# Loading x in three groups of blocks, with a norm for each group, in a two-layer decoder trunk

## The chip, the cores and the metric

The kernel runs on one core of one Trainium2 chip. The core has five engines with instruction streams of their own: TensorE (PE; its weight loads are shown as PEld), VectorE (DVE), ScalarE (ACT), GpSimd (POOL) and SyncE (SP, which here only issues DMAs). Each engine takes its instructions in the order in which they stand in its stream and waits on semaphores for the others. The metric is the time of one execution on the device, in microseconds; lower is better.

## The reference

One inference step of a trunk of two layers, for a prompt of 1024 positions and a decode batch of 8, with 1024 features. Layer 0 mixes with a gated linear recurrence (HGRN2), layer 1 with sliding-window attention; each layer has a SwiGLU feed-forward part. Every sub-layer is modulated by a conditioning vector `c`. What matters here is the very start: norm, modulation and first projection of layer 0.

```
def modulate(x, g, shift, scale):
    y = rms_norm(x, g) * (1.0 + scale[:, None, :]) + shift[:, None, :]
def ada_params(c, w, b):
    return (jax.nn.silu(c) @ w + b).astype(jnp.float32)
...
sh1, sc1, g1, sh2, sc2, g2 = jnp.split(ada_params(c, w_ada[l], b_ada[l]), 6, axis=-1)
xn = modulate(h, norm_w[l, 0], sh1, sc1)
...
q, f_raw, i, g = jnp.split(xn @ w_in, 4, axis=-1)      # the first projection, 1024 -> 4096
```

## The kernel before

**Tiling.** The 1024 prompt positions and the 8 decode positions stand side by side as 1032 columns; features lie on the 128 partitions, in `KT` = 8 row tiles `k`. For the first projection the columns are cut into three chunks `c` of 344 (`G3`). x is loaded in eight blocks of 128 positions, `xt[0]` to `xt[7]` (`load_x`, L380), and turned on PE into the feature-major tiles `h[k]` (`turn_x`, L451: per `k` one transpose for each block, then one DVE copy, L457, out of the bank).

**First norm.** ACT squares each block and sums it (`first_square`, L861). DVE makes one over the root by `newton` (L540, eleven small instructions behind the one of L887), puts the results on a diagonal (`dg`, L891), PE multiplies that by ones (L907) so that every partition has the factor of each column, and ACT copies it to `N.R` (L908). Before, this is done once for all eight blocks.

**Conditioning.** Shift and scale of layer 0 come from `w_ada`, loaded as 16 tiles of 512 KB in two halves: `wa[0]` gives them for the row tiles 0 to 3, `wa[1]` for 4 to 7. `first_step(i, k)` (L498) multiplies one tile, two matmuls; `first_end(i)` (L512) copies the result (L514), transposes it (L517) and leaves shift and scale in `ada` and `modA` (L522 to L530).

**Rows.** `N.apply_steps` (L732) makes the modulated input of one chunk, row tile by row tile: DVE L738, ACT L742 (high part), DVE L743 (low part). High and low parts are tiles of `X` (16 of them). Each `next` on it does two row tiles; a chunk's first four therefore need `wa[0]` alone.

**Projection.** Weights are streamed in units of 512 KB (`Stream`, `split_unit`, L191). A unit is loaded into one of three `raw` buffers and converted in two halves by `weight` (L179): ACT casts the high part (L182), POOL subtracts to get the low part (L185). For the first four units the conversion is held back (`held`) and called by hand. Units 0 to 3 are the four parts (f, v, q, g) of head 0. Each product is three matmuls (`mm3`, L282 to L285): high by high, high by low, low by high. In `hgrn_first` (L963) `part(c, i)` is unit `i` for chunk `c` over the first four row tiles, twelve matmuls; its accumulator stays in a PSUM bank, of tag `mm` or, for (1, 0) and (1, 1), of tag `ax`. Six parts are done this way, then, with the second conditioning half, the rest.

**What sets the order.** A planner puts the instructions of each engine in an order: it goes by the order of the text, but lets a later instruction go first where it holds the earlier one to be not ready yet. Three things bind it. `tc.keep_in_program_order(i)` pins an instruction behind the one that stands before it in the text on the same engine; the casts L182 of the first four units are pinned so. Buffers of one tag are handed out in the order of the text of the tiles' first instructions: a tile of a later line gets its buffer only after all the tiles of that tag from earlier lines have theirs. The tags here are `c4` (34 buffers of about 4 KB a partition: x blocks, `wa`, `h`, `X`), `raw` (3), `mm` (4 PSUM banks) and `ax` (4 PSUM banks). And DMAs of SP go through eight semaphores in turn, so that an issue waits for the landing of the one eight before it.

Before, x blocks 0 to 2 are loaded, then 3 to 7, then unit 0, the eight tiles of `wa[0]`, units 1 and 2, and four tiles of `wa[1]`; the other four follow at L899, where `turn_x(6, 2)` has been done and a `c4` buffer is free.

Of the kernel before, what the change touches and what calls it, by code (L numbers as in the profile page):

```python
# [57 lines left out]
def bc(ap, axis, n):  # L58
    u = ap.unsqueeze(axis)
    shape = list(u.shape)  # L60
    shape[axis] = n
    return u.to_broadcast(shape)
# [3 lines left out]
def trunk_kernel(  # L66
# [313 lines left out]
    def load_x(tb):  # L380
        t = big(cols=D)
        sp.dma_start(t, x_prompt[0, tb * P : (tb + 1) * P, :])
        xt.append(t)
# [8 lines left out]
    act.dma_start(pr2[40:48, :], final_norm_w.rearrange("(k f) -> k f", f=P))  # L392
    act.dma_start(pr2[48:56, :], lb_a.rearrange("l (k f) -> (l k) f", f=P))
    act.dma_start(pr2[56:57, :], gnorm_a)
    for tb in range(3, 8):
        load_x(tb)


    def first_half(k, i, t):
        src = w_ada[0][k * P : (k + 1) * P, 0:2048].rearrange("p (s n) -> p s n", s=2)  # L400
        sp.dma_start(t.rearrange("p (s n) -> p s n", s=2), src[:, :, i * 512 : (i + 1) * 512])
        return t
# [3 lines left out]
    for kk in range(4):  # L406
        t = big(cols=1024)
        wa[0].append(first_half(2 * kk, 0, t))
        t = big(cols=1024)
        wa[0].append(first_half(2 * kk + 1, 0, t))  # L410
    ws.ahead(3)
    for k in range(4):
        t = big(cols=1024)
# [37 lines left out]
    def turn_x(t0, n):  # L451
        for k in range(KT):
            ps = mmp() if k % 2 else axp()
            for j in range(n):
                pe.transpose(ps[:, j * P : (j + 1) * P], xt[t0 + j][:, k * P : (k + 1) * P], ident)
            dst = h[k][:, t0 * P : (t0 + n) * P]
            dve.tensor_copy(dst, ps[:, : n * P])  # L457

# [399 lines left out]
    dve.memset(ms, 1.0)  # L858

    def first_square(tb):  # L860
        act.activation(junk[:, :T], xt[tb], AF.Square, accum_out=ms[:, tb : tb + 1])  # L861

    act.activation(junk[:NB, :T], xd_in, AF.Square, accum_out=ms[:NB, 8:9])
    for tb in range(3):
        first_square(tb)
    turn_x(0, 3)
    for tb in range(3, 6):
        first_square(tb)
    turn_x(3, 3)
    for tb in range(6, 8):  # L870
        first_square(tb)
    held.pop(0)()


# [9 lines left out]
    dve.tensor_tensor(lb, lbe, lbe, op=ALU.subtract)  # L884
    dve.tensor_scalar(omlb, lb, -1.0, 1.0, op0=ALU.mult, op1=ALU.add)

    dve.tensor_scalar(ms, ms, 1.0 / D, EPS, op0=ALU.mult, op1=ALU.add)  # L887
    newton(y, ms, 9, P, "n")
    for half in range(2):
        s = slice(512 * half, 512 * half + 512)  # L890
        dve.tensor_tensor(  # L891
            dg[:, s].rearrange("p (j q) -> p j q", j=4),
            bc(ident, 1, 4),
            bc(y[:, 4 * half : 4 * half + 4], 2, P),
            op=ALU.mult,
        )
    dve.tensor_tensor(dg[:NB, T:TOK], ident[:NB, :NB], y[:NB, 8:9].to_broadcast([NB, NB]), op=ALU.mult)
    turn_x(6, 2)
    for k in range(4, KT):  # L899
        wa[1].append(first_half(k, 1, big(cols=1024)))  # L900
    ws.ahead(4)
    for k in range(2):
        first_step(0, k)
    for half in range(2):
        s = slice(512 * half, 512 * half + 512)
        ps = axp()
        pe.matmul(ps, ones, dg[:, s], start=True, stop=True)  # L907
        act.copy(N.R[:, s], ps)  # L908
    ps = axp()
    pe.matmul(ps[:, :NB], ones[:NB, :], dg[:NB, T:TOK], start=True, stop=True)  # L910
    act.copy(N.R[:, T:TOK], ps[:, :NB])
    for k in range(2, KT):
        first_step(0, k)
    first_end(0)
    X = Rows(KT)
    steps = [N.apply_steps(c, 0, X) for c in range(NCH)]
    held.pop(0)()
    for c in range(2):
        for _ in range(2):
            next(steps[c])  # L920
        if c == 0:
            held.pop(0)()


    osc = dp.tile([NH, P, T], F32, name="osc")
    odec = cst.tile([P, NH, NB], F32, name="odec")
# [34 lines left out]
            yield from ada_end(hh)  # L961

    def hgrn_first():  # L963
        us = ws.done[:4]
        acc = {}

        def part(c, i):
            acc[c, i] = axp() if c and i < 2 else mmp()
            proj(acc[c, i][:, :W], us[i], X, c, 0, 4)

        for c, i in ((0, 0), (0, 1), (0, 2), (1, 0)):
            part(c, i)
        for k in range(KT):
            first_step(1, k)
        part(1, 1)
        first_end(1)
        part(1, 2)
        held.pop(0)()
        for st in steps:
            for _ in st:  # L980
                pass
        for _ in us:
            ws.next()
        f, kk, v, q, g = (big() for _ in range(5))
        for c in range(NCH):
            s = G3.all(c)
            for i, t in enumerate((f, v, q, g)):
                ps = acc.get((c, i))
                if ps is None:
                    ps = mmp()  # L990
                    proj(ps[:, :W], us[i], X, c)
                else:
                    proj(ps[:, :W], us[i], X, c, 4, KT)
                if t is v:
                    act.copy(t[:, s], ps[:, :W])
                else:
                    act.activation(t[:, s], ps[:, :W], AF.Sigmoid)
                if t is q or t is g:
                    dve.tensor_tensor(t[:, s], t[:, s], ps[:, :W], op=ALU.mult)
        forget(0, f, kk)  # L1000
        data[0] = [f, kk, v, q, g]
        yield
# [1049 lines left out]
```

## Time and profile before

| | |
|---|---|
| time, three runs | 2525.5, 2527.67 and 2528.7 us; median 2527.67 |
| profiled execution | 2529.57 us, of which the span from the first to the last instruction is 2527.8 |
| mean granted TensorE clock | 0.992 |
| moved by DMA | 293.41 MB, mean 116 GB/s |
| read from HBM, written to it | 231.27 MB, 63.99 MB |

The profile shows one execution. Times are in microseconds from the first instruction. In the timeline a row has its start, its length, the engine, the line, the operation, what it writes and reads, shapes, and in brackets how long the engine had been idle and what ended that. `SPq` is SyncE issuing DMAs. Buffer numbers are left out: `c` stands for tiles of tag `c4`, `wu` for converted weights. Rows of the same line that follow each other without a gap are merged, with their count (`x8`). PE counts an fp32 matmul as several instructions.

### The profile page before, as it was taken

Reading aid. Unit: us, or ns where it says so; the run is one execution under the profiler, and the core shown is the slowest. Engines: PE = TensorE matmul, PEld = TensorE weight load, DVE = VectorE, ACT = ScalarE, POOL = GpSimd, SP = SyncE. Lnnn points to the kernel's source line nnn. Section 1 sums busy time; section 2 is a strip of 40 time slices with the busy share of each in tenths; the row PEclk is TensorE's granted clock in tenths of the full one; section 3 lists DMA queues with packets and bytes.
Section 4 is the critical chain, followed back from the end, with each engine's and each line's share of the span. In section 5 each row is a group of like instructions: output and inputs, shape, how many; then the busy total and the mean of one; then the engine's idle time right before and its main releaser. Section 6 shows DMA issues by size and latency. Waiting matters only on the chain.

```text
span 2527.8 us, 52251 instructions
## 1 busy us (share of the span) xinstructions
PE 2469.5 (98%) x21579; PEld 2346.0 (93%) x21579; DVE 1366.9 (54%) x3117; ACT 878.7 (35%) x1929; POOL 797.3 (32%) x577
## 2 busy tenths in 40 slices
PE   7999999999999999999999999999899999999998
PEld 4989999987889999999999997878899999999998
DVE  5444555564574555656433725566845555555436
ACT  4323333331363332333211655454633333333112
POOL 2211222220334444444432231102334444445321
PEclk9999999999999999999999999999999999999999
DMA  8564222248942223226321322523222222264201
GB/s 317 188 213 138 72 78 69 69 149 286 284 126 78 81 85 116 89 89 229 123 76 54 89 55 59 155 88 109 76 70 82 84 76 76 76 230 145 69 26 68
DMA packets 314495, 293.41 MB, mean 116 GB/s; under 512 B 28617, under 2 KB 291674, under 8 KB 314226
## 3 DMA queue, kind: packets, MB, share of 16 engines
q1 hardware_dynamic: 313856, 289.86, 35.5%
q8 instruction: 170, 2.79, 0.4%
q14 instruction: 67, 0.55, 0.1%
q10 hardware_dynamic: 402, 0.22, 0.0%
HBM read 231.27 MB, written 63.99 MB: 117 GB/s over the span
## 4 chain that ended last, share of the span: by engine, by line
PE 89%; DVE 5%; DMA 2%; issue 2%; SPq 1%; ACT 0%; POOL 0%; DVEq 0%; POOLq 0%; ACTq 0%
PE mm L283 20%; PE mm L285 20%; PE mm L284 20%; PE ax L283 6%; PE ax L284 6%; PE ax L285 6%; PE ax L473 2%; PE ax L1798 1%; PE ax L1869 1%; PE ax L1043 1%; PE ax L1855 1%; DVE c L1064 1%; PE ax L1132 1%; PE ax L1169 1%; DVE hs L809 1%
## 5 line engine op out<-in xcount | busy, mean ns | idle before, releaser
L185 POOL TENSOR_TENSOR wu<-raw,wu 128x512 fp32r<-128x512 f32 x460 | 626.2, 1368 | 1354.8 <-ACT wu L182 1118.7
L283 PE MATMUL mm<-c,wu 128*128 128x344 f32 (+1 forms) x2096 | 669.9, 320 | 6.0 <-ACT c L742 4.1
L285 PE MATMUL mm<-c,wu 128*128 128x344 f32 (+1 forms) x2096 | 658.7, 314 | 1.7 <-POOL wu L185 1.7
L284 PE MATMUL mm<-c,wu 128*128 128x344 f32 (+1 forms) x2096 | 658.7, 314 | 0.1
L182 ACT CAST wu<-raw 128x512 fp32r<-128x512 f32 x460 | 283.3, 620 | 705.9 <-PE mm L285 377.0
L283 PEld LDWEIGHTS mm<-c,wu 128*128 128x128 f32 x2096 | 395.6, 189 | 20.0 <-issue 10.3
L283 PE MATMUL mm<-xq,wu 128*128 128x258 f32 x1448 | 412.2, 285 | 1.0 <-ACT wu L182 1.0
L285 PE MATMUL mm<-xq,wu 128*128 128x258 f32 x1448 | 409.9, 283 | 0.8 <-POOL wu L185 0.8
L284 PE MATMUL mm<-xq,wu 128*128 128x258 f32 x1448 | 410.3, 283 | 0.0
L285 PEld LDWEIGHTS mm<-c,wu 128*128 128x128 f32 x2096 | 395.6, 189 | 6.2 <-issue 4.1
L284 PEld LDWEIGHTS mm<-c,wu 128*128 128x128 f32 x2096 | 396.2, 189 | 4.3 <-issue 3.4
L283 PE MATMUL ax<-xq,wu 128*128 128x258 f32 x1064 | 301.4, 283 | 0.0
L284 PE MATMUL ax<-xq,wu 128*128 128x258 f32 x1064 | 300.9, 283 | 0.0
L285 PE MATMUL ax<-xq,wu 128*128 128x258 f32 x1064 | 300.6, 283 | 0.0
L285 PEld LDWEIGHTS mm<-xq,wu 128*128 128x128 f32 x1448 | 275.2, 190 | 2.3 <-issue 1.2
L283 PEld LDWEIGHTS mm<-xq,wu 128*128 128x128 f32 x1448 | 274.5, 190 | 2.0 <-ACT wu L182 1.2
L284 PEld LDWEIGHTS mm<-xq,wu 128*128 128x128 f32 x1448 | 275.4, 190 | 0.1
L844 DVE SCALAR_TENSOR_TENSOR hs<-mm,ada,hs 128x344 f32<-128x344 f32 (+3 forms) x228 | 120.5, 532 | 183.8 <-PE mm L285 170.8
L284 PEld LDWEIGHTS ax<-xq,wu 128*128 128x128 f32 x1064 | 202.3, 190 | 0.0
L285 PEld LDWEIGHTS ax<-xq,wu 128*128 128x128 f32 x1064 | 201.6, 190 | 0.0
L283 PEld LDWEIGHTS ax<-xq,wu 128*128 128x128 f32 x1064 | 201.0, 189 | 0.0
L844 DVE SCALAR_TENSOR_TENSOR c<-mm,ada,c 128x344 f32<-128x344 f32 (+1 forms) x132 | 74.9, 571 | 111.3 <-PE mm L285 110.6
(323 smaller groups left out, 3596.1 us busy)
## 6 DMA issues: line engine op xcount, KB each, us to landing
c<-in_w_ada_dram SPq DMA_DIRECT2D x96, 512.0 KB
raw<-in_w_ffn_in_dram SPq DMA_DIRECT2D x152, 256.0 KB
ff<-c SPq DMA_DIRECT2D x44, 516.0 KB
c<-ff SPq DMA_DIRECT2D x44, 516.0 KB
raw<-in_w_ffn_out_dram SPq DMA_DIRECT2D x44, 512.0 KB
raw<-in_w_in_a_dram SPq DMA_DIRECT2D x32, 512.0 KB
hs<-hs SPq DMA_DIRECT2D x16, 516.0 KB
out_dram<-c SPq DMA_DIRECT2D x16, 512.0 KB
```

What stands on the lines that cost most here:

```text
L182: i = act.copy(u[:, 0, :], src)
L185: eng.tensor_tensor(u[:, 1, :], src, u[:, 0, :], op=ALU.subtract)
L283: pe.matmul(ps, wh, xh, start=first, stop=False)
L284: pe.matmul(ps, wh, xl, start=False, stop=False)
L285: pe.matmul(ps, wl, xh, start=False, stop=last)
L473: pe.matmul(ada_ps[q][32 * j : 32 * j + 32, 256 * i : 256 * i + 256], cT[:, k, :], u[i][:, j, :], start=(k == 0 and i == 0), stop=(k == KT ...
L809: dve.tensor_tensor(t, t, bc(R, 1, t.shape[1]), op=ALU.mult)
L844: dve.scalar_tensor_tensor(hc, ps[:, : g.pl[c]], ada[:, gate + n, 0:1], hc, op0=ALU.mult, op1=ALU.add)
L1043: pe.matmul(ps[32 * j : 32 * j + 32, c * 32 : (c + 1) * 32], KS[:, t0 : t0 + 32], QP[:, t0 : t0 + 32], start=True, stop=True, tile_positio ...
L1064: dve.tensor_tensor(q4[:, :, 1, :], q4[:, :, 1, :], bc(p3[:, :, 0], 2, M), op=ALU.mult)
L1132: pe.matmul(ps[:, j * P : (j + 1) * P], kt[:, s], vt[:, s], start=True, stop=True)
L1169: pe.matmul(o, attT[:, c, :], vt[:, s], start=(c == 0), stop=True)
```

## The change

x is loaded in three groups: blocks 0 to 2, 3 to 5, 6 and 7. Behind the first group come unit 0 and the eight `wa[0]` tiles; the second group stands behind those, then unit 1, the third group, unit 2 and the first four tiles of `wa[1]`. Each group gets its squares, its transposes and a norm of its own (`first_rows`, which replaces L863 to L871 and L887 to L911 with the same instructions on fewer columns): group one at the old place, group two behind the first four rows of chunk 0, group three inside `hgrn_first`, behind `part(0, 1)`. In groups two and three the squares and transposes are pinned with `keep_in_program_order`. Unit 1 is converted behind the second group's norm, unit 2 behind the third's, and the last four tiles of `wa[1]` and unit 3 are loaded behind that. All eight `first_step(0, k)` stand together. The decode positions' factor is made with the third group. What is computed is the same.

```diff
@@ -392,8 +392,6 @@
     act.dma_start(pr2[40:48, :], final_norm_w.rearrange("(k f) -> k f", f=P))
     act.dma_start(pr2[48:56, :], lb_a.rearrange("l (k f) -> (l k) f", f=P))
     act.dma_start(pr2[56:57, :], gnorm_a)
-    for tb in range(3, 8):
-        load_x(tb)
 
 
     def first_half(k, i, t):
@@ -408,6 +406,11 @@
         wa[0].append(first_half(2 * kk, 0, t))
         t = big(cols=1024)
         wa[0].append(first_half(2 * kk + 1, 0, t))
+    for tb in range(3, 6):
+        load_x(tb)
+    ws.ahead(2)
+    for tb in range(6, 8):
+        load_x(tb)
     ws.ahead(3)
     for k in range(4):
         t = big(cols=1024)
@@ -452,7 +455,9 @@
         for k in range(KT):
             ps = mmp() if k % 2 else axp()
             for j in range(n):
-                pe.transpose(ps[:, j * P : (j + 1) * P], xt[t0 + j][:, k * P : (k + 1) * P], ident)
+                i = pe.transpose(ps[:, j * P : (j + 1) * P], xt[t0 + j][:, k * P : (k + 1) * P], ident)
+                if t0:
+                    tc.keep_in_program_order(i)
             dst = h[k][:, t0 * P : (t0 + n) * P]
             dve.tensor_copy(dst, ps[:, : n * P])
 
@@ -858,17 +863,39 @@
     dve.memset(ms, 1.0)
 
     def first_square(tb):
-        act.activation(junk[:, :T], xt[tb], AF.Square, accum_out=ms[:, tb : tb + 1])
+        return act.activation(junk[:, :T], xt[tb], AF.Square, accum_out=ms[:, tb : tb + 1])
 
     act.activation(junk[:NB, :T], xd_in, AF.Square, accum_out=ms[:NB, 8:9])
-    for tb in range(3):
-        first_square(tb)
-    turn_x(0, 3)
-    for tb in range(3, 6):
-        first_square(tb)
-    turn_x(3, 3)
-    for tb in range(6, 8):
-        first_square(tb)
+
+    def first_rows(t0, n):
+
+
+        for tb in range(t0, t0 + n):
+            i = first_square(tb)
+            if t0:
+                tc.keep_in_program_order(i)
+        turn_x(t0, n)
+        dec = t0 + n == 8
+        w = n + dec
+        v, yv = ms[:, t0 : t0 + w], y[:, t0 : t0 + w]
+        dve.tensor_scalar(v, v, 1.0 / D, EPS, op0=ALU.mult, op1=ALU.add)
+        newton(yv, v, w, P, "n")
+        s = slice(t0 * P, (t0 + n) * P)
+        dve.tensor_tensor(
+            dg[:, s].rearrange("p (j q) -> p j q", j=n), bc(ident, 1, n), bc(yv[:, :n], 2, P), op=ALU.mult
+        )
+        ps = axp()
+        pe.matmul(ps[:, : n * P], ones, dg[:, s], start=True, stop=True)
+        act.copy(N.R[:, s], ps[:, : n * P])
+        if dec:
+            dve.tensor_tensor(
+                dg[:NB, T:TOK], ident[:NB, :NB], y[:NB, 8:9].to_broadcast([NB, NB]), op=ALU.mult
+            )
+            ps = axp()
+            pe.matmul(ps[:, :NB], ones[:NB, :], dg[:NB, T:TOK], start=True, stop=True)
+            act.copy(N.R[:, T:TOK], ps[:, :NB])
+
+    first_rows(0, 3)
     held.pop(0)()
 
 
@@ -884,43 +911,17 @@
     dve.tensor_tensor(lb, lbe, lbe, op=ALU.subtract)
     dve.tensor_scalar(omlb, lb, -1.0, 1.0, op0=ALU.mult, op1=ALU.add)
 
-    dve.tensor_scalar(ms, ms, 1.0 / D, EPS, op0=ALU.mult, op1=ALU.add)
-    newton(y, ms, 9, P, "n")
-    for half in range(2):
-        s = slice(512 * half, 512 * half + 512)
-        dve.tensor_tensor(
-            dg[:, s].rearrange("p (j q) -> p j q", j=4),
-            bc(ident, 1, 4),
-            bc(y[:, 4 * half : 4 * half + 4], 2, P),
-            op=ALU.mult,
-        )
-    dve.tensor_tensor(dg[:NB, T:TOK], ident[:NB, :NB], y[:NB, 8:9].to_broadcast([NB, NB]), op=ALU.mult)
-    turn_x(6, 2)
-    for k in range(4, KT):
-        wa[1].append(first_half(k, 1, big(cols=1024)))
-    ws.ahead(4)
-    for k in range(2):
-        first_step(0, k)
-    for half in range(2):
-        s = slice(512 * half, 512 * half + 512)
-        ps = axp()
-        pe.matmul(ps, ones, dg[:, s], start=True, stop=True)
-        act.copy(N.R[:, s], ps)
-    ps = axp()
-    pe.matmul(ps[:, :NB], ones[:NB, :], dg[:NB, T:TOK], start=True, stop=True)
-    act.copy(N.R[:, T:TOK], ps[:, :NB])
-    for k in range(2, KT):
+    for k in range(KT):
         first_step(0, k)
     first_end(0)
     X = Rows(KT)
     steps = [N.apply_steps(c, 0, X) for c in range(NCH)]
+    for _ in range(2):
+        next(steps[0])
+    first_rows(3, 3)
     held.pop(0)()
-    for c in range(2):
-        for _ in range(2):
-            next(steps[c])
-        if c == 0:
-            held.pop(0)()
-
+    for _ in range(2):
+        next(steps[1])
 
     osc = dp.tile([NH, P, T], F32, name="osc")
     odec = cst.tile([P, NH, NB], F32, name="odec")
@@ -961,15 +962,21 @@
             yield from ada_end(hh)
 
     def hgrn_first():
-        us = ws.done[:4]
         acc = {}
 
         def part(c, i):
             acc[c, i] = axp() if c and i < 2 else mmp()
-            proj(acc[c, i][:, :W], us[i], X, c, 0, 4)
-
-        for c, i in ((0, 0), (0, 1), (0, 2), (1, 0)):
-            part(c, i)
+            proj(acc[c, i][:, :W], ws.done[i], X, c, 0, 4)
+
+        part(0, 0)
+        part(0, 1)
+        first_rows(6, 2)
+        held.pop(0)()
+        for k in range(4, KT):
+            wa[1].append(first_half(k, 1, big(cols=1024)))
+        ws.ahead(4)
+        part(0, 2)
+        part(1, 0)
         for k in range(KT):
             first_step(1, k)
         part(1, 1)
@@ -979,8 +986,7 @@
         for st in steps:
             for _ in st:
                 pass
-        for _ in us:
-            ws.next()
+        us = [ws.next() for _ in range(4)]
         f, kk, v, q, g = (big() for _ in range(5))
         for c in range(NCH):
             s = G3.all(c)
```

## The prediction

> **What bounds the kernel now.** I read the page first, then busy time by stretch, then the timeline.
>
> ```profile
> span 2527.8 us, 52251 instructions
> ...
> PE 2469.5 (98%) x21579; PEld 2346.0 (93%) x21579; DVE 1366.9 (54%) x3117; ACT 878.7 (35%) x1929; POOL 797.3 (32%) x577
> ...
> PE 89%; DVE 5%; DMA 2%; issue 2%; SPq 1%; ACT 0%; POOL 0%; DVEq 0%; POOLq 0%; ACTq 0%
> ```
>
> TensorE carries the span. An edit of the start can only shorten or lengthen the time in which PE has nothing to do. The stretches (length, then busy time of PE, PEld, DVE, ACT, POOL, the granted clock, DMA share, GB/s):
>
> ```profile
> 9.20:24.50 15.30, 14.49 (x86) 10.22 (x85) 13.61 (x36) 12.65 (x22) 2.50 (x2) 1.00 1.03 389
> 24.50:38.40 13.90, 7.09 (x26) 1.96 (x26) 5.63 (x18) 3.40 (x8) 3.37 (x3) 1.00 0.90 306
> 38.40:46.22 7.82, 6.07 (x26) 5.41 (x26) 6.65 (x14) 4.57 (x9) 5.33 (x2) 0.78 0.64 221
> 46.22:59.12 12.90, 12.20 (x82) 8.70 (x83) 2.44 (x6) 2.26 (x5) 3.74 (x3) 1.00 1.00 340
> 59.12:100.00 40.88, 40.77 (x260) 40.45 (x261) 21.09 (x50) 21.55 (x48) 9.88 (x8) 1.00 0.40 141
> ```
>
> From 59.12 on PE has no gap, so what counts is how early that state is reached, with how much work done. The way there, in the timeline:
>
> ```profile
> 9.65 9.01 SPq L401 DMA_DIRECT2D c<-in_w_ada_dram  x8
> 30.14 1.05 PE L503 MATMUL ax<-c,cT 128*32 128x512 f32 x4 [0.26 <-DMA c<-in_w_ada_dram]
> 33.68 0.60 ACT L514 COPY c<-ax 128x512 f32<-128x512 f32 x1
> 36.23 2.48 DVE L738 SCALAR_TENSOR_TENSOR w<-c,modA,c 128x344 f32<-128x344 f32 x3
> 38.40 0.90 PE L283 MATMUL mm<-c,wu 128*128 128x344 f32 x2 [3.41 <-ACT c L742]
> 46.22 0.42 PE L285 MATMUL mm<-c,wu 128*128 128x344 f32 x1 [1.75 <-POOL wu L185]
> 47.91 0.32 PE L283 MATMUL ax<-c,wu 128*128 128x344 f32 x1
> 49.64 0.32 PE L285 MATMUL ax<-c,wu 128*128 128x344 f32 x1
> 49.89 4.12 PE L503 MATMUL ax<-c,cT 128*32 128x512 f32 x32
> 59.12 0.74 PE L283 MATMUL mm<-c,wu 128*128 128x344 f32 x3 [0.70 <-ACT c L742]
> 59.97 0.42 PE L284 MATMUL mm<-c,wu 128*128 128x344 f32 x1
> ```
>
> The first conditioning half waits for its eight tiles until 30.14; projections start at 38.40; the second half's matmuls run at 49.89; its X rows reach PE at 59.12. One `part` is twelve matmuls, 47.91 to 49.64 for eleven steps, so 1.9 us. Between 59.12 and 59.97 three matmuls run where that pace allows 5.4: the gapless state counts from 59.5.
>
> **The change, part by part.** *Loads.* Five x blocks (512 KB each) go behind the eight tiles. At 389 GB/s they are 6.7 us, so the last tile lands at 23.4 and its matmuls (1.05) end at 24.5. L514 to the first L738 is 2.55 (33.68 to 36.23). L514 no longer stands behind the norm's copies (2.5, from 31.19), since group one's norm is done while tiles load. First L738 at 27.0, against 36.23: this is the change's gain, 9.2 us at this point.
>
> *What is queued behind it now.* Before, all eight squares, copies and the norm ran under the load wait. Now five blocks' work follows. Prices:
>
> ```profile
> 10.16 1.06 ACT L861 ACTIVATE c<-c 128x1024 f32<-128x1024 f32 x1
> 18.44 1.06 ACT L861 ACTIVATE c<-c 128x1024 f32<-128x1024 f32 x1
> 14.82 0.56 DVE L457 COPY c<-mm 128x384 f32<-128x384 f32 x1
> 18.54 0.54 DVE L457 COPY c<-mm 128x384 f32<-128x384 f32 x1
> 19.01 0.41 DVE L457 COPY c<-ax 128x256 f32<-128x256 f32 x1
> 20.33 0.41 DVE L457 COPY c<-ax 128x256 f32<-128x256 f32 x1
> 23.36 0.15 DVE L550 SCALAR_TENSOR_TENSOR nt<-ny 128x9 f32<-128x9 f32 x1
> 24.97 0.17 DVE L552 SCALAR_TENSOR_TENSOR ny<-nt,ny 128x9 f32<-128x9 f32 x1
> 25.25 0.69 DVE L891 TENSOR_TENSOR c<-ident,ny 128x512 f32<-128x512 f32 x1
> 31.12 1.98 PE L907 MATMUL ax<-c,ones 128*128 128x512 f32 x4
> 32.28 0.59 ACT L908 COPY c<-ax 128x512 f32<-128x512 f32 x1 [10.14 <-PE ax L907]
> 41.07 0.56 DVE L738 SCALAR_TENSOR_TENSOR w<-c,modA,c 128x344 f32<-128x344 f32 x1
> 43.02 2.03 DVE L743 SCALAR_TENSOR_TENSOR c<-w,ada,c 128x344 fp32r<-128x344 f32 x4
> 40.88 6.53 POOL L185 TENSOR_TENSOR wu<-raw,wu 128x512 fp32r<-128x512 f32 x2 [2.63 <-ACT wu L182]
> 20.18 2.50 POOL L185 TENSOR_TENSOR wu<-raw,wu 128x512 fp32r<-128x512 f32 x2 [18.41 <-ACT wu L182]
> ```
>
> Start to start: a square 1.18 (seven steps, 10.16 to 18.44); a three-block copy 0.465 (eight, 14.82 to 18.54), eight of them 3.7; a two-block copy 0.33 (four), eight 2.6; a norm's chain 0.20 a step (eight, 23.36 to 24.97), twelve steps 2.4; the diagonal 0.69 per 512 columns; its matmul half of 1.98 per 512; its copy 0.59. Four rows of X are eight DVE instructions, 41.07 to 45.05: 4.0.
>
> Estimates from these, in order, on DVE unless said: rows of chunk 0 to 31.0; copies of blocks 3 to 5 to 34.7 (their squares are pinned behind the fourth L742, three times 1.18, and are covered); norm and diagonal 2.9 to 37.6; matmul 0.75 and copy 0.45 to 38.8; rows of chunk 1 to 42.8.
>
> The weights are pinned too:
>
> ```profile
> 19.49 1.12 ACT L182 CAST wu<-raw 128x512 fp32r<-128x512 f32 x2
> 34.16 1.16 ACT L182 CAST wu<-raw 128x512 fp32r<-128x512 f32 x2
> 25.49 6.03 SPq L401 DMA_DIRECT2D c<-in_w_ada_dram  x4
> 34.88 2.48 POOL L185 TENSOR_TENSOR wu<-raw,wu 128x512 fp32r<-128x512 f32 x2 [12.20 <-ACT wu L182]
> 37.30 0.95 POOL L928 MEMSET c<- 128x1024 f32 x1
> 39.99 2.53 SPq L401 DMA_DIRECT2D c<-in_w_ada_dram  x4
> ```
>
> Unit 0's cast waited for the last square, unit 1's for L514. Now unit 1's cast stands behind the second norm's copy (38.8) and unit 2's behind the third. Unit 1's POOL half then meets chunk 1's rows on DVE. Before, that meeting took 6.53 for two passes against 2.50 alone, and `part` (0,2) got its half only at 46.22, 1.2 after DVE stopped (45.05). So (0,1) gets its half at 44.0 and ends at 45.6 (ten matmuls, 1.6). Blocks 6 and 7 are pinned behind (0,1) on PE and behind chunk 1's fourth L742 on ACT: a first transposed pair 0.2 later, copies end at 48.4, norm and diagonals (2.9) at 51.3, matmuls (0.7) at 52.0. R for the last chunk is not needed at once.
>
> The second conditioning half cannot slip ahead. Buffers of a tag go out in the order of the text: L928 has no input, yet POOL, idle 12.20 before unit 1's pass, runs it only after that, at 37.30, behind X's sixteen tiles; the first four second-half tiles were issued from 25.49, yet L503 came at 49.89, behind (1,0), which takes the `ax` bank before it. In the changed text (1,0) and that bank stand behind the third norm's two `ax` banks. So from 52.0 PE still has (0,2), (1,0), the half's 4.1, (1,1), four transposes (0.4) and (1,2): 12.1 us, gapless, to 64.1. The next rows come beside it: 52.0+1.9+4.1+2.55 is 60.6 for L738, 2.2 more (36.23 to 38.40) to PE, 62.8. At 59.5 before, all of that was done.
>
> *Clock.* PE would idle about 4.0 us before 52.0. The only idle time here that halved the clock is the 5.0 before 38.40 (0.78 over 7.82, so 1.7 lost); the 0.70 before 59.12 did not. The price lies between 0 and 1.7; 4.0 is nearer to 5.0, so 1.7. The Trainium skill ("TensorE: Matmul & The Clock Gate", section on HAM oscillation) warns of idle gaps above some 3.4 us; by that rule this change adds three such gaps, and without it the sum would be 1.7 lower.
>
> *At no cost.* On SP, units 1 and 2 now stand between x groups. At 512 KB in 1.35 us (389 GB/s), blocks 3 to 5 land at 27.4, unit 1 at 28.8, blocks 6 and 7 at 31.5, unit 2 at 32.8; they are wanted at 31.0, 38.8, 45.6 and 52, so the waits above cover them; without that cover each would delay its step by its lateness. The last four second-half tiles are issued later in the text, behind L928's buffer. The SP rows show four issues at 39.99 to 42.5, their matmuls done by 54.0; here they are needed at about 56. Cover gone, each microsecond late costs one. The two extra norms' instructions (24 at 0.2) are in the chain above. The x, tile and weight bytes are the same. Unknown: where the planner puts the copies of blocks 3 to 5 against chunk 0's rows. If some come first, they wait for x on the queue: 0 to 1 us; taken 0, since the text has the rows first.
>
> **Sum.** 64.1 minus 59.5, plus 1.7: 6.3 later. Span 2527.8 gives 2534.1; the profiled execution took 2529.57, above the median of 2527.67 by 1.9, which I leave out: **2534.0 us**.
>
> **Rivals.** *A, the waits overlap.* POOL gets its pass in early, as at 20.18 (1.25 a pass): (0,1) ends before 43, DVE alone sets the third norm: 42.8+1.25+2.6+2.9 gives 49.6, matmuls 50.3, PE idles little, 62.4: plus 2.9, 2530.6. Against it stands the 6.53. The Trainium skill ("SBUF — State Buffer", "Who interferes with whom") has VectorE and GpSimd lock each other out for one whole instruction; by it POOL would wait for one DVE instruction, 0.56, not for a run of them, which is this rival; the 6.53 speaks against it.
>
> *B, faster.* The half's matmuls are let into PE's gaps. Its eight tiles, at 1.35 each behind unit 2 (32.8), can be on chip by 43.6; DVE, after blocks 6 and 7 (42.8+2.6+2.9), starts chunk 0's second rows at 48.3, PE at 50.5, with (0,2) and (1,2) left, 3.8: 54.3, 5.2 earlier than 59.5: 2522.5. Against it: 49.89 behind (1,0), while PE sat idle for 3.41 before 38.40.
>
> *C, slower still.* SP's idle time is filled with the second cache copy, so the last four tiles land late: this decides once they land after 56. One more such copy (1 MB each way, 340 GB/s) is 6 us on 53, so 59, some 3 past the need at 56: 2537.
>
> That the first projection does not follow the first group is possible (its `mm` bank waits for a copy of blocks 3 to 5, to about 32), and costs nothing.
>
> **Numbers.** Forecast 0.52 (own range 2531 to 2537), A 0.25, B 0.10, C 0.13. Range 2527.5 to 2539.5: it leaves out B and the far end of C. What a measurement can tell is 0.2%, 5.1 us, so 2522.6 to 2532.7 is no change: of the forecast 0.08 lies below 2532.7, of A nearly all (0.23), of B 0.02, being at the edge. Faster 0.08, same 0.33, slower 0.59.
>
> **What would show it.** First L738 near 27 and first L283 at 28 to 32; squares of blocks 6 and 7 after 42; L182 of unit 1 right behind a norm's copy; PE idle before the third norm's matmul; L503 of the second half after 52. L503 before the third norm, or gapless PE before 59, would make it wrong.

## The result, and the profile after

The changed kernel took 2543.23 us (median of four runs, 2542.12 to 2543.57), against 2526.59 for the kernel before beside it (four runs, 2525.11 to 2528.70): ratio 1.0064, 95% interval 1.0047 to 1.0082. That is slower, as forecast, but by 16.6 instead of 6.3, and outside the range. In the profiled execution the span is 2541.8 against 2527.8, 14.0 longer. Of the runs below, one execution of the kernel before (8177 us) and one of the kernel with filled gaps (8374 us) took more than three times as long and are left out of the medians and ratios.

First the stretches of the changed kernel (columns as in the prediction: length, busy time of PE, PEld, DVE, ACT, POOL, granted clock, DMA share, GB/s).

```profile
9.20:24.50 15.30, 11.38 (x60) 6.49 (x63) 8.33 (x28) 7.39 (x13) 3.46 (x3) 0.78 1.05 392
38.40:46.22 7.82, 5.96 (x19) 4.38 (x18) 6.19 (x9) 5.09 (x10) 3.15 (x2) 0.50 0.67 233
46.22:59.12 12.90, 9.23 (x38) 7.88 (x37) 5.46 (x23) 2.31 (x6) 2.52 (x2) 0.68 0.59 190
70.00:80.00 10.00, 7.78 (x32) 7.72 (x33) 9.30 (x19) 5.55 (x10) 1.18 (x1) 0.66 0.73 270
```

Before, PE had no gap from 59.12 on. Here it is without one only from 72.22, and the clock was halved four times on the way: the trace's clock records put it at 0.50 from 16.84 to 23.66, 37.32 to 47.56, 50.97 to 57.80 and 71.45 to 78.28, 30.7 us in all, where the kernel before had 3.4. Most lines that matter here have moved by five: L738 is L743 now, L742 is L747, L457 is L462, L503 is L508, L514 is L519, L517 is L522. The norm's matmul L907 is L888. The start, from the timeline:

```profile
18.14 1.62 PE L888 MATMUL ax<-c,ones 128*128 128x384 f32 x2 [3.92 <-DVE c L884]
19.69 5.59 PE L508 MATMUL ax<-c,cT 128*32 128x512 f32 x32
27.13 0.55 DVE L462 COPY c<-ax 128x384 f32<-128x384 f32 x1
28.16 1.54 DVE L743 SCALAR_TENSOR_TENSOR w<-c,modA,c 128x344 f32<-128x344 f32 x3
29.40 0.43 PE L283 MATMUL mm<-c,wu 128*128 128x344 f32 x1
37.84 1.65 PE L888 MATMUL ax<-c,ones 128*128 128x384 f32 x2 [4.13 <-DVE c L884]
38.70 0.83 SPq L1269 DMA_DIRECT2D out_dram<-in_cache_swa_k_dram  x1
39.64 2.61 SPq L399 DMA_DIRECT2D c<-in_w_ada_dram  x4
40.03 4.08 DVE L743 SCALAR_TENSOR_TENSOR w<-c,modA,c 128x344 f32<-128x344 f32 x4 [2.25 <-ACT c L889]
40.59 3.15 POOL L185 TENSOR_TENSOR wu<-raw,wu 128x512 fp32r<-128x512 f32 x2 [16.21 <-ACT wu L182]
42.28 0.65 PE L285 MATMUL mm<-c,wu 128*128 128x344 f32 x1 [0.77 <-POOL wu L185]
44.04 2.03 DVE L748 SCALAR_TENSOR_TENSOR c<-w,ada,c 128x344 fp32r<-128x344 f32 x4
51.87 1.22 PE L888 MATMUL ax<-c,ones 128*128 128x256 f32 x2 [3.55 <-DVE c L884]
53.54 0.66 PE L283 MATMUL ax<-c,wu 128*128 128x344 f32 x1
```

PE waits 3.92 for the first norm, and the norm and most of the first conditioning half behind it run at half clock: 5.59 for the half's 32 matmuls, 4.12 or less at full clock. The first projection starts at 29.40, nine earlier than before. Then PE waits twice more for a norm, 4.13 and 3.55, and the third norm's matmul starts at 51.87, where 52.0 was forecast for its end. Up to here the forecast holds to 1.5. What follows does not:

```profile
59.70 1.92 PE L508 MATMUL ax<-c,cT 128*32 128x512 f32 x16
61.56 0.42 PE L283 MATMUL ax<-c,wu 128*128 128x344 f32 x1
65.50 1.92 PE L508 MATMUL ax<-c,cT 128*32 128x512 f32 x16
67.52 0.59 ACT L519 COPY c<-ax 128x512 f32<-128x512 f32 x1 [12.67 <-PE ax L508]
68.16 0.66 PE L522 MATMUL ax<-ident,c 128*128 128x128 f32 x4 [0.73 <-ACT c L519]
72.22 1.23 PE L283 MATMUL mm<-c,wu 128*128 128x344 f32 x3 [3.41 <-ACT c L747]
73.25 0.49 PE L284 MATMUL mm<-c,wu 128*128 128x344 f32 x1
78.13 0.39 PE L285 MATMUL mm<-c,wu 128*128 128x344 f32 x1
```

The second conditioning half runs in two pieces. Between them, from 61.56 to 65.50, stand (1,1) and (1,2), the 24 matmuls that were to cover the making of the second rows. When the last piece ends, PE has nothing left: it waits 0.73 and 3.41, and then runs at half clock (0.49 a matmul, against 0.32) until 78.13. No wait stands in the brackets of the second piece at 65.50, so the tiles were there: by the trace's semaphore events the last four had landed whole at 48.4, 50.0, 51.3 and 52.6, before even the first piece. It is the order of PE's stream, fixed when the program was built, that puts this piece last.

How much work was late is best read from a count. The view of stretches, narrowed to PE's matmuls with converted weights over the first 100 us, gives for before and after (length, busy time with the count, clock, DMA share, GB/s):

```profile
0.00:100.00 100.00, 54.14 (x323) 0.98 0.69 242
```

```profile
0.00:100.00 100.00, 45.29 (x231) 0.85 0.64 229
```

92 matmuls fewer, at the 0.157 a matmul of the gapless stretch (eleven steps in 1.73), are 14.4 us: the span's 14.0. At 80 us the difference is already 98 (202 against 104), so the whole loss is made by then, and the count at 100 us serves as the measure of each experiment below. It is good to 1 or 2 us: shortly before 100 us the kernels that are ahead run other matmuls too (before from 95.49), which take up to 1.9 from it.

### The profile page after: what moved, and what is told of

It is laid out like the page before. It is cut to its first block, busy times and chain, and to the rows that moved or that the text cites. A ratio compares the mean times of both kernels' runs of the same rounds, so it can differ in the third digit from the quotient of the medians.

```text
span 2541.8 us, 52284 instructions
## 1 busy us (share of the span) xinstructions
PE 2474.5 (97%) x21581; PEld 2350.5 (92%) x21581; DVE 1379.3 (54%) x3142; ACT 879.2 (35%) x1930; POOL 794.7 (31%) x577
## 4 chain that ended last, share of the span: by engine, by line
PE 89%; DVE 6%; issue 2%; DMA 1%; ACT 0%; ACTq 0%; POOL 0%; DVEq 0%; SPq 0%; POOLq 0%
PE mm L283 20%; PE mm L285 20%; PE mm L284 20%; PE ax L283 6%; PE ax L285 6%; PE ax L284 6%; PE ax L478 2%; PE ax L1804 1%; PE ax L1875 1%; PE ax L1049 1%; PE ax L1861 1%; DVE c L1070 1%; PE ax L1138 1%; PE ax L1175 1%; DVE hs L849 1%
```

## The experiments

The theory, **order**: the cache copy issued at 38.70 stands ahead of the last four second-half tiles; the planner therefore takes these for late and puts their matmuls behind (1,1) and (1,2); this costs the wait before 72.22 and the half clock behind it, some 7 us of the 14. The first rival, **chain**: three norms made one after the other, on DVE and POOL, cost it all. The second, **loads**: the tiles were late by themselves.

| kernel | median, us | ratio to before, 95% interval | matmuls in 100 us | late by, us |
|---|---|---|---|---|
| before | 2526.59 | 1 | 323 | 0 |
| after | 2543.23 | 1.0064 (1.0047 to 1.0082) | 231 | 14.4 |
| half held whole | 2536.80 | 1.0038 (1.0025 to 1.0051) | 279 | 6.9 |
| last tiles loaded early | 2543.01 | 1.0061 (1.0049 to 1.0073) | 226 | 15.2 |
| cache copies late | 2535.11 | 1.0035 (1.0023 to 1.0047) | 265 | 9.1 |
| three norms alone | 2548.50 | 1.0083 (1.0070 to 1.0096) | 204 | 18.7 |
| load order alone | 2533.46 | 1.0021 (1.0012 to 1.0031) | 289 | 5.3 |
| half whole, gaps filled | 2535.46 | 1.0035 (1.0022 to 1.0048) | 290 | 5.2 |
| before, gap filled | 2526.93 | 1.0000 (0.9992 to 1.0009) | 319 | 0.6 |
| half ahead of third group | 2528.70 | 1.0010 (1.0001 to 1.0020) | 307 | 2.5 |
| the same, unit 2 early | 2524.54 | 0.9991 (0.9982 to 1.0000) | 338 | -2.4 |
| the same once more | 2523.77 | 0.9994 (0.9984 to 1.0004) | 337 | -2.2 |
| before, norm in the load wait | 2527.89 | 1.0001 (0.9992 to 1.0011) | 324 | -0.2 |

The last column is the difference from 323, times 0.157. Each ratio is to runs of the kernel before on the same chip.

### The half held whole

```diff
     def mm3(ps, wh, wl, xh, xl, first, last):
-        pe.matmul(ps, wh, xh, start=first, stop=False)
+        i = pe.matmul(ps, wh, xh, start=first, stop=False)
+        if pin[0]:
+            tc.keep_in_program_order(i)
+        pin[0] = False
...
             acc[c, i] = axp() if c and i < 2 else mmp()
+            pin[0] = (c, i) in ((1, 1), (1, 2))
```

> The changed kernel, with the first matmul of (1,1) and of (1,2) held in text order on PE, so that the second conditioning half runs as one block ahead of them. Theory, order: the changed kernel loses time because half of that block runs behind (1,1) and (1,2), so that nothing is left on PE while the second rows of X are made. Then here the half runs from about 59.7 to 63.6, L519 comes at about 63.7 instead of 67.52, the rows reach PE at about 68.4 instead of 72.22 with at most 1 us idle ahead of them, the granted clock of 70 to 80 is 1.00 instead of 0.66, and the span falls from 2541.8 to 2535 to 2536.5. Rival, chain: the three norms in series made the whole loss and the order is of no account: span 2541 to 2543. Rival, loads: the last four tiles are late: the matmuls wait for them on PE with a DMA named as the cause, span 2541 or more.

Measured: span 2535.8, ratio 1.0038. From its timeline, and its stretch from 70 to 80 (L513 is L508 here):

```profile
58.19 3.64 PE L513 MATMUL ax<-c,cT 128*32 128x512 f32 x32
66.98 0.75 PE L285 MATMUL mm<-c,wu 128*128 128x344 f32 x3 [0.75 <-ACT c L752]
70.00:80.00 10.00, 10.00 (x65) 10.00 (x65) 9.90 (x22) 8.12 (x16) 0.00 (x0) 1.00 0.95 388
```

One block of 3.64, (1,1) and (1,2) behind it, and only 0.75 of idle time before the rows arrive; the clock stays at 1.00. The count rises from 231 to 279, 7.5 us, of which 1.5 was there before the block (58.19 for 59.70); 0.9 of this the first row already had (27.27 for 28.16), behind a first half-clock stretch of 3.4 where the changed kernel had 6.8. Chain and loads both expected nothing here: the order makes some 6 of the 14. What is left puts the time, 2536.80, inside the range that the prediction gave for the whole change.

### The last tiles loaded early

```diff
     ws.ahead(3)
-    for k in range(4):
+    for k in range(KT):
         t = big(cols=1024)
         wa[1].append(first_half(k, 1, t))
...
-        for k in range(4, KT):
-            wa[1].append(first_half(k, 1, big(cols=1024)))
```

> The changed kernel, with the loads of the last four second-half tiles written right behind the first four. Theory, order: they are issued at about 29 ahead of the small sink loads and the cache copy, the block runs whole without being held, and the span is that of the kernel with the block held, 2535 to 2536.5. Rival, loads: it is faster than that kernel by 2 us or more, since the tiles' landing mattered by itself. Rival, chain: 2541 to 2543.

Missed: 1.0061, no better than the change. The block did run whole, as expected, and the rows arrived early; the loss came later:

```profile
58.91 3.64 PE L508 MATMUL ax<-c,cT 128*32 128x512 f32 x32
67.12 0.74 PE L283 MATMUL mm<-c,wu 128*128 128x344 f32 x3
75.20 8.24 POOL L185 TENSOR_TENSOR wu<-raw,wu 128x512 fp32r<-128x512 f32 x2 [18.84 <-ACT wu L182]
82.27 0.65 PE L285 MATMUL mm<-c,wu 128*128 128x344 f32 x1 [5.70 <-POOL wu L185]
```

Now unit 3's load stands behind the cache copy, and its conversion is put behind the second rows, at 74.52 on ACT instead of 62.41 with the block held, though the unit had landed at 53.5. The reading is that it is taken for late in its turn; this run does not show that by itself, but in the kernel with the copies late, below, the conversion is back at 64.63. Beside the rows POOL got little room: two passes that take 2.5 alone took 8.24, and PE waited 5.70. One item had been exchanged for the next behind the same copy.

### The cache copies late

```diff
-        sp.dma_start(ck_sample[:, 0 : WIN - 1], cache_swa_k[:, 1:WIN])
-        sp.dma_start(cv_sample[:, 0 : WIN - 1], cache_swa_v[:, 1:WIN])
+        tc.keep_in_program_order(sp.dma_start(ck_sample[:, 0 : WIN - 1], cache_swa_k[:, 1:WIN]))
+        tc.keep_in_program_order(sp.dma_start(cv_sample[:, 0 : WIN - 1], cache_swa_v[:, 1:WIN]))
```

> The changed kernel, its text untouched but for the two cache copies, which are held at their own place far behind the start of SP's queue instead of filling its idle time. Theory, copies: it is the cache copy issued at 38.70 ahead of the last four second-half tiles that makes the planner take these tiles for late, and so put their matmuls behind (1,1) and (1,2). Then here the block of the half runs whole with no hold on PE, the rows reach PE near 67 to 68, and the span is that of the kernel with the block held, 2535 to 2536.5. Rival, the order comes from elsewhere: two blocks of the half as before, span 2541 to 2543.

```profile
60.42 3.64 PE L508 MATMUL ax<-c,cT 128*32 128x512 f32 x32
69.19 0.74 PE L283 MATMUL mm<-c,wu 128*128 128x344 f32 x3 [0.73 <-ACT c L747]
```

Measured: span 2533.3, ratio 1.0035. With no hold on PE the block is whole. This names the cause of the order in the changed kernel: the copy in SP's idle time, an instruction that has nothing to do with the change. (The rows reached PE at 69.19, later than expected; this execution was late already at the second norm's matmul, 38.51 for the 36.95 of the kernel with the block held. Their times do not tell the two apart.) In the kernel before, the same copy stands ahead of the same four tiles, and the block was whole all the same. Why the planner judged otherwise there was not tried.

### Each part alone

The three norms with the loads as before:

```diff
+    for tb in range(3, 8):
+        load_x(tb)
...
-    for tb in range(3, 6):
-        load_x(tb)
-    ws.ahead(2)
-    for tb in range(6, 8):
-        load_x(tb)
     ws.ahead(3)
```

> The changed kernel with the loads in the order of before: x whole, then units 0 to 2, then the first-half tiles; the three norms stay. Theory, chain: the first half's matmuls end near 31.2 instead of 25.3, the first L743 comes near 33.9 instead of 28.16, and all behind it moves by as much, since each group's work is written behind the rows of the one before: span about 2547.5 (2546 to 2549). Rival, the norms are free once x is there early: span below 2535.

The loads of the change in the kernel before, with its one norm: the same lines the other way round.

> The kernel before with the loads in the changed order alone; one norm over all blocks as before. Theory, chain: the one norm now waits for x blocks 6 and 7 (landed near 31.5), PE runs their transposes ahead of the first half's matmuls, first L738 near 41 instead of 36.23, span 2527.8 plus 4 to 6: 2532 to 2534. Rival, the early tiles alone are a gain: span below 2526. Rival, nothing: 2526 to 2530.

Measured: 1.0083 (span 2545.3) and 1.0021 (span 2531.7), both slower, and each a little less than expected (the spans lie 0.7 and 0.3 below their ranges). With the norms alone the first row came at 32.43, 4.3 later than in the change, and the count fell by another 27 matmuls, 4.2 us: each group's work stands behind the rows of the one before, so a late first row moves all. With the loads alone the one norm waits for the last x blocks:

```profile
42.94 2.48 DVE L741 SCALAR_TENSOR_TENSOR w<-c,modA,c 128x344 f32<-128x344 f32 x3
```

The first row is at 42.94 instead of 36.23, 6.7 later, and 5.3 of that arrives at the count. Neither part of the change is a gain by itself.

### The gaps filled

To price the half clock, idle PE time was filled with matmuls whose result is overwritten; once in the kernel with the block held, once in the kernel before.

```diff
         ps = axp()
+        for _ in range({3: 24, 6: 11}.get(t0, 0)):
+            tc.keep_in_program_order(pe.matmul(ps[:, :P], ones, ident, start=True, stop=True))
         pe.matmul(ps[:, : n * P], ones, dg[:, s], start=True, stop=True)
```

> The kernel with the block of the half held whole, and idle PE time filled with matmuls of 128 by 128 whose result is overwritten: 24 ahead of the second norm's matmul, 11 ahead of the third's. Theory, clock: the idle gaps of 4.1 and 3.6 halve the granted clock behind them, and that is on the path: the second norm's matmul takes about 0.85 instead of 1.65, the third's 0.6 instead of 1.2, twenty-four matmuls behind it 3.8 instead of 5.2; the clock is 0.95 or more in 38.40 to 59.12 and the span falls from 2535.8 by 3 to 4, to 2532 to 2533. Rival, the slow matmuls lie beside other waits: the clock is full and the span falls by less than 1.5.

> The kernel before, with 11 such matmuls ahead of the first projection, in the idle 3.4 before 38.40. Theory, clock: the 1.7 that the halved clock behind 38.40 costs comes back: clock 0.95 or more over 38.40 to 46.22, span 2526 (2525.5 to 2526.8). Rival: DVE's rows and unit 2's low half, not PE, set that stretch: 2527.3 to 2528.5.

The rows below are from one more execution of the first of the two:

> The kernel with filled gaps once more, for a profile at the usual clock. It gained nothing against the kernel with the block whole (ratio to before 1.0035 against 1.0038). Theory 1, the filling did not keep the clock: half-speed matmuls are still seen in 38 to 59. Theory 2, it kept the clock, but the slow matmuls had lain beside other waits: clock 0.95 or more there, and the idle time is longer ahead of the third norm's matmul. Either way a span near 2534.

```profile
37.49 0.91 PE L895 MATMUL ax<-c,ones 128*128 128x384 f32 x2 [1.29 <-DVE c L889]
50.88 0.70 PE L895 MATMUL ax<-c,ones 128*128 128x256 f32 x2 [0.94 <-DVE c L889]
46.22:59.12 12.90, 11.59 (x86) 8.77 (x88) 4.48 (x20) 1.52 (x4) 2.52 (x2) 0.97 0.69 223
65.21 0.74 PE L285 MATMUL mm<-c,wu 128*128 128x344 f32 x3 [0.72 <-ACT c L752]
```

The norms' matmuls are at full speed (0.91 for 1.65, 0.70 for 1.22) and the clock of 46.22 to 59.12 is 0.97 instead of 0.74. Over 38.40 to 46.22 it stayed at 0.61, where 0.95 was expected: waits of 1.29, 1.09 and 1.12 were left there, and half clock followed from 40.2 to 47.0. Of 17.1 us at half clock between 24 and 60 the filling took away 10.2. The rows reach PE at 65.21 instead of 66.98: 1.8 gained of the 3 to 4 expected, 1.7 by the count, too little for the times to show. (This one execution took 2540.12, span 2538.3 for the expected 2534, so only its start is read.) That the rest of those slow matmuls lay beside waits for POOL and DVE fits the shorter gain, but was not shown on its own, and what the half clock that was left costs stays open.

In the kernel before, the filling gained nothing (1.0000), but it did not hold the clock either: half clock had lain from 38.5 to 41.9, and now lay from 40.9 to 47.7, twice as long. So this run gives no price.

### The half ahead of the third group

If what is left is idle PE time under the second and third norm, then work that is ready must be put there. This kernel loads all second-half tiles and unit 3 ahead, holds the copies late, converts unit 1 right behind unit 0, and changes the order:

```diff
         part(0, 0)
         part(0, 1)
-        first_rows(6, 2)
-        held.pop(0)()
...
-        part(0, 2)
-        part(1, 0)
         for k in range(KT):
             first_step(1, k)
+        part(1, 0)
         part(1, 1)
         first_end(1)
+        first_rows(6, 2)
+        held.pop(0)()
+        part(0, 2)
         part(1, 2)
```

> The changed kernel's three norms and loads, in another order of work: all second-half tiles and unit 3 loaded ahead of the sink loads, the cache copies held late, unit 1 converted right behind unit 0, and on PE the half, (1,0) and (1,1) ahead of the third group of x. Theory, series: what remains of the loss once the half runs whole (about 8 on the span) is idle PE time while the second and third norm are made, and work for it was there: the half starts near 38.5, and the state that was reached at 59.5 before is reached at 56 to 58, span 2524 to 2527. Rival, the norms themselves cost DVE too much: 2530 or more.

Measured: span 2528.3, 1.0010. The loss is gone but for 2.5 by the count; the half starts at 39.53. The 2524 to 2527 expected was missed in this execution, and the timeline says where:

```profile
38.69 0.91 PE L890 MATMUL ax<-c,ones 128*128 128x384 f32 x2 [2.92 <-DVE c L886]
39.53 3.89 PE L510 MATMUL ax<-c,cT 128*32 128x512 f32 x28
53.85 0.58 PE L283 MATMUL mm<-c,wu 128*128 128x344 f32 x2 [2.06 <-ACT c L749]
```

PE waits 2.06 for the second rows, with (0,2) and (1,2) still held by unit 2's conversion behind the third norm, and half clock follows (54.3 to 61.1; 0.81 over 46.22 to 59.12). So unit 2's `held.pop(0)()` was moved behind chunk 1's rows, and (0,2) and (1,2) ahead of `first_rows(6, 2)`:

> The kernel with the half first, with unit 2 converted right behind chunk 1's rows and (0,2) and (1,2) on PE ahead of the third group's transposes, so that PE has work while the second rows and the third norm are made. Theory, series: the 2.06 that PE waits before 53.85 and the half clock of 54 to 61 in that kernel go; from 39 PE is busy over 95%, clock 0.95 or more over 46.22 to 70; by about 55.5 the work is done that was done at 59.5 before: span 2523 to 2525, below the kernel before. Rival, DVE: with both rows' groups, the copies and the third norm on it at 50 to 60, DVE becomes the bound: PE waits for L748 and the span stays 2527 to 2530.

```profile
38.40:46.22 7.82, 7.82 (x45) 3.30 (x46) 4.08 (x8) 4.92 (x9) 1.71 (x2) 0.78 0.51 161
46.22:59.12 12.90, 12.90 (x87) 12.55 (x86) 9.83 (x34) 7.77 (x15) 0.84 (x1) 1.00 0.42 134
0.00:100.00 100.00, 57.42 (x338) 0.98 0.69 238
```

PE is gapless from 38.4 to 59.1, DVE does not bind it, and 338 matmuls are done in 100 us, 15 more than before. Span 2521.4, below the 2523 to 2525 expected; ratio 0.9991, interval to 1.0000. It was run once more beside the last kernel:

> The kernel with unit 2 early, beside the one above on one chip. First measurement: 0.9991 of before, interval 0.9982 to 1.0000. If it is a real gain of its start (3.7 at the 288th projection matmul), the ratio is again 0.9980 to 0.9992; if it was the spread of the runs, 0.9995 or more.

0.9994, just outside the band expected for a real gain and short of the one for none, with an interval that takes in 1. The start gained 2.2 to 2.4 us by the count in both profiles (3.1 to 3.3 at 80 us, 20 and 21 matmuls ahead); both medians, 2524.54 and 2523.77, lie 2.7 to 2.9 below those of before beside them. It is the fastest kernel here and 0.7% faster than the change, but against the kernel before one interval only just reaches 1 and the other includes it.

### Before, with the norm under the load wait

The one gain that the change surely had is that L514 no longer waits for the norm's copies. It can be had without the rest:

```diff
-    for k in range(2):
+    for k in range(4):
         first_step(0, k)
...
-        pe.matmul(ps, ones, dg[:, s], start=True, stop=True)
+        tc.keep_in_program_order(pe.matmul(ps, ones, dg[:, s], start=True, stop=True))
...
-    for k in range(2, KT):
-        first_step(0, k)
+    for k in range(4, KT):
+        first_step(0, k, pin=k == 4)
```

> The kernel before, with the norm's matmuls and copies on PE and ACT behind the first eight of the first half's sixteen matmul pairs, that is, under the wait for the tiles, instead of behind all of them. This does alone the one thing that the change was seen to gain for certain: L514 no longer waits for the norm's copies. Theory: L514 starts at about 31.3 instead of 33.68 and the first L738 at about 33.9 instead of 36.23, and as DVE, POOL and the weights follow, the start of the 288th projection matmul comes 1.5 to 2.4 before its 93.56: time 0.9990 to 0.9994 of before. Rival: unit 2's low half or the second half's tiles hold the stretch before 59.12 as they are, and the gain is lost by there: 0.9998 to 1.0002.

```profile
30.32 0.58 ACT L516 COPY c<-ax 128x512 f32<-128x512 f32 x1 [1.54 <-PE ax L503]
32.86 2.48 DVE L740 SCALAR_TENSOR_TENSOR w<-c,modA,c 128x344 f32<-128x344 f32 x3
48.23 1.05 PE L503 MATMUL ax<-c,cT 128*32 128x512 f32 x4 [0.61 <-DMA c<-in_w_ada_dram]
52.38 1.05 PE L503 MATMUL ax<-c,cT 128*32 128x512 f32 x4 [0.53 <-DMA c<-in_w_ada_dram]
```

The first row came 3.4 earlier (32.86), more than expected, and the time did not move: 1.0001. PE reached the second half at 45.70 instead of 49.89, and now waited there tile by tile until 52.38 for the same last four tiles. What was expected of the rival happened. Here, not in the change, these tiles are late in truth.

## Why the prediction was wrong, point by point

Right: the change makes it slower; PE's gapless state decides; the first rows come 8.1 and the first projection nine earlier, and the gain is used up by five blocks' work behind them. *What is queued behind it now* holds: second norm's copy done at 38.8 by the forecast and 40.0 as measured, third norm's matmuls at 52.0 and 53.6.

*Loads* came out near, 27.0 forecast and 28.16 measured for the first row, in part by luck. The last tile landed at 21.88, not 23.4. Its matmuls could have ended near 22.9 (21.88 + 1.05, an estimate), not at 24.5; but half clock followed the wait for the first norm, and they ended at 25.28 (19.69 + 5.59). The forecast had no such term. The two copies of blocks 3 to 5 that went ahead of the rows cost only 0.2: from L519 (25.38) to the first row were 2.78, for the 2.55 of before.

Rival A was half right. POOL did get in early (3.15 for its two passes, where 6.53 had been set against it), but DVE was slowed beside it: chunk 1's eight instructions took 6.0 (40.03 to 46.07) instead of 4.0. (0,1) had its half at 42.28 instead of 44.0, and the third norm was no earlier. That the one holds the shared SBUF port for a whole instruction, and the other waits, is what the Trainium skill states ("SBUF — State Buffer", "Who interferes with whom"). At 40.03 the trace roughly agrees: four rows of 0.49 and two passes of 1.25, one after the other, would be 4.5, and the four rows took 4.08.

**The step that failed** is in the paragraph that begins "The second conditioning half cannot slip ahead": "from 52.0 PE still has (0,2), (1,0), the half's 4.1, (1,1), four transposes (0.4) and (1,2): 12.1 us, gapless, to 64.1", with the rows hidden at 62.8. That order was taken from the text. In PE's stream half of the block stood behind (1,2), so nothing covered the rows: they came at 72.22, 4.1 after the 68.1 that the whole block would have given (59.70 + 3.64 for the block, then the 4.7 from L519 to the matmul at 72.22 as measured), and another 2.8 went to half clock (21 matmuls from 72.22 to 78.4, 6.1 where the gapless pace is 3.3). With the block whole the kernel lost 6.9 and 9.1 by the count, in the two ways it was made so.

The cover was thinner than that sum said, too. Its order puts two parts, (0,2) and (1,0), ahead of the half, but "52.0+1.9+4.1+2.55" counts one. With both, L738 comes at 62.5 and the rows reach PE at 64.7, some 0.6 after 64.1. With the block whole PE did wait 0.75 there, and 0.73 with the copies late.

*At no cost* had the right place and the wrong way of asking. It said that the last four tiles are needed at 56 and that "each microsecond late costs one". They had landed by 52.6, and they cost seven all the same, because the order had been fixed when the program was built. That it was fixed on a wrong estimate of their landing is what the kernel with the copies late speaks for. Rival C named SP's idle time and a cache copy, but a real lateness: 2537, by too little.

*Clock* was mis-sized: 1.7 for one gap, where four waits, of 3.92, 4.13, 3.55 and 3.41, each had half clock behind them. The row that the term rested on was misread as well: the 5.0 before 38.40 are two waits, 0.92 and 3.41, with 0.66 of transposes between them. The half clock fell on the first conditioning half (above), on (0,2) and (1,0), 53.54 to 59.70, 6.2 for 3.8 (some 0.3 of it a wait for unit 2's low half), and on the norms' matmuls (1.65 for 0.91, 1.22 for 0.70, by the filled kernel), besides the 2.8 above. What was shown of it on the path is 1.8 (the filled gaps) in the kernel with the block whole. The Trainium skill ("TensorE: Matmul & The Clock Gate", section on HAM oscillation) warns of idle gaps above some 3.4 us. By that rule the prediction had counted three such gaps, and in that it was nearer than the row of before by which the term was set.

The pieces add up roughly: 1.5 at the third norm (53.54 for 52.0), 2.4 on (0,2) and (1,0), 4.1 for the rows and 2.8 behind them are 10.8; less the 1.7 that had been put in for the clock, 9.1 above the forecast, against 8.1 by the count and 7.7 by the spans.

## What to carry to other kernels

Where an order is fixed on estimates, ask of each transfer not only when it lands but when the planner believes it lands: a copy of no importance, parked in a queue's idle time, reorders the work behind it, and loading one item earlier hands the harm to the next. An earlier start was worth nothing here while the next supplier was no earlier (3.4 gained at the first row, 0 at the end), and splitting a step into stages cost time until each wait that it made had ready work of another stage put into it; even then the gain was hardly more than the runs can tell. Price every gap of the engine that bounds the kernel twice, for its length and for the clock behind it.

## What was not expected of the hardware

The half clock comes in whole steps. In stretches of 1 us of the changed kernel the granted clock changes within these:

```profile
37.00:38.00 1.00, 0.17 (x1) 0.17 (x2) 0.72 (x2) 0.00 (x0) 0.00 (x0) 0.66 0.05 9
47.00:48.00 1.00, 1.00 (x9) 1.00 (x8) 0.99 (x3) 0.00 (x0) 0.00 (x0) 0.72 0.98 343
...
71.00:72.00 1.00, 0.00 (x0) 0.00 (x0) 1.00 (x3) 0.41 (x1) 0.18 (x1) 0.72 0.00 0
78.00:79.00 1.00, 1.00 (x8) 1.00 (x6) 1.00 (x3) 0.00 (x0) 0.00 (x0) 0.86 1.05 430
```

A mean of 0.66 over 37 to 38 is a change to 0.50 at 37.32; likewise 47.56, 71.45 and 78.28. The half clock lasts 10.24 and 6.83, and from the first of these points to the last are 40.96: three, two and twelve times 3.41. The first change, at 16.84, lies 18 such steps before the last. The half clock was 3.4 long in the kernel before and 6.8 in the one with the half first. So in these runs the clock changes on a fixed grid of some 3.41, and what a gap does goes by how it falls on it: the same wait of 2.9 ahead of the second norm's matmul was followed by no half clock with the half first (28 of the half's matmuls in 3.89), and by a step of it in the kernel with unit 2 early:

```profile
38.34 0.91 PE L890 MATMUL ax<-c,ones 128*128 128x384 f32 x2 [2.91 <-DVE c L886]
39.18 5.34 PE L510 MATMUL ax<-c,cT 128*32 128x512 f32 x32
```

Run once more, the same kernel had the same wait (2.92) and full clock behind it. It gained nothing by that: the half now caught up with the landing of its last tiles, waited 0.18 and 0.33 for them, and the next part began at 44.53, for 44.45 with the half clock. A slow stretch is free where the work in it would have waited anyway.

The Trainium skill ("TensorE: Matmul & The Clock Gate", Part 1) states a free-running window of 3413 ns, with which these numbers agree; its advice to avoid gaps above 3.4 us is not enough here, since half clock also followed waits of 2.06 and 2.91.

GpSimd's passes beside VectorE's rows took 3.15 with DVE slowed, or 8.24 with DVE at its usual 0.5 a row, for the same two passes of 2.5. Which of the two engines pays differed from place to place, and no run here shows what decides it.
